# The output projection of the last layer in token parts of 384 and 136, with shorter roots and unused matmuls ahead of the last spread

## The chip, the cores and the metric

The kernel runs on one core of a Trainium2 chip. The metric is the device time of one execution in microseconds (us). Three runs of the kernel before took 1245.64, 1245.87 and 1247.6 us, median 1245.87. Each trace comes from one execution, taken by the hardware profiler.

Names of the engines: PE is the tensor engine's matmuls, PEld its weight loads, DVE the vector engine, ACT the scalar engine, POOL GpSimd, SP the engine that issues most DMAs.

## The reference, cut to what matters

Two layers (`DEPTH = 2`), `D_MODEL = 1024`, 512 prompt tokens and 8 decode samples of one token. Each layer is

```python
mod = jax.nn.silu(c) @ w_ada + b_ada
shift, scale, gate = jnp.split(mod[:, None, :], 3, axis=-1)
h = rmsnorm(x, norm_w) * (1.0 + scale) + shift
proj = h @ w_in                      # 1024 -> 7 * 1024
...
merged = jax.nn.sigmoid(gm) * y_m + jax.nn.sigmoid(gc) * y_c
x = x + gate * (merged @ w_out)
```

with an mLSTM branch (`y_m`) and a causal convolution branch (`y_c`) between. After the second layer a last `rmsnorm(x, final_norm_w)` gives the outputs for prompt and samples:

```python
def rmsnorm(x, w):
    xf = x.astype(jnp.float32)
    r = lax.rsqrt(jnp.mean(xf * xf, axis=-1, keepdims=True) + EPS)
    return (xf * r).astype(x.dtype) * w
```

## The kernel before, in words

Everything is held feature-major: a tile has 128 features on the partitions and the 520 tokens (512 prompt tokens, then the 8 samples) along the free axis; `KT = 8` such tiles make the 1024 features.

*Dense products.* `dense` (L178) makes one output tile of 128 features: for each of two token halves of 260 (`HALF`) it runs, over the 8 input tiles, three matmuls into one PSUM bank. Three, because weights and activations are split in a high and a low part of type fp32r (`whi`, `wlo`; `mh`, `ml` in the last stage), and high x high, high x low and low x high are summed. Each matmul is 128x128 weights by 260 columns, and each loads its weights anew. `split_w` (L161) brings a pair of weight tiles by DMA (`raw`, two buffers), casts the high part on ACT and subtracts the low part on POOL in four pieces of 256 columns. High and low land in rotating buffers (`WB = 3`), or in given places.

*Order.* The program is written in stages; a scheduler that simulates the engines sets each engine's order, within the dependencies and some `issue_after` hints. An engine runs its instructions in that order and waits at the first whose inputs are missing.

*The last stage* (`last_out`, L334) is the output projection of the second layer together with the final norm. For each output tile `m` and half `c`, `half` (L342) runs the 24 matmuls, adds the gated product to the old `x` on DVE (`residual`, L323; for the second half the samples need two more small instructions), squares on ACT, adds the squares up over the tiles on POOL (`presum`, into `total`) and multiplies by the norm weight on ACT. The tiles 0 to 3 run both halves in turn. The tiles 4 to 7 run their first halves first, then their second halves, so that the first half's norm can be made and written while the second halves are multiplied (`M_SPLIT = 4`). Since tiles 4 and 5 are used twice at a distance, their weights lie in buffers of the tag `k`, which the step before frees (`place`, L380).

*The norm of a half.* For the last tile the squares and `total` are summed over the partitions by matmuls with ones into four groups of 32 partitions (L352, `rmsn`), so that each instruction of the root works on 65 columns instead of 260. `inv_rms` (L357) scales the sum on DVE and takes the root: `rsqrt` (L149) starts with an integer guess and makes three Newton steps of three instructions. With the scaling (`var`) the root is eleven DVE instructions. `spread` (L362) brings the four groups back to all partitions with four matmuls (`frb`; fp32 matmuls appear as two records each) and copies the result to SBUF on ACT (`rbs`). `write` (L371) multiplies six tiles on DVE from PSUM and two on POOL from SBUF, and SP writes them to `o_y` in pairs. The pair (4, 5) of the first half is multiplied on DVE only after the last residual.

*Other uses of the root.* `rstd_of` (L224) calls it with 130 columns for the norm at the start of each layer (spread: `rb`) and for the convolution branch's layer norm (`lrb`); `norm_scales` calls it with 17 columns for the heads' norms of the mLSTM.

*The start.* While the first weights arrive, the sums of the first norm (`rms`) and the modulation `w_ada` (`ada`, chunks of four weight pieces that come one after the other by DMA, turned by `adat`) run on PE. Twelve unused matmuls of the identity (`idle`, L431) stand behind the first spread `rb`.

Of the kernel before, what the change touches and what calls it, by code (L numbers as in the profile page):

```python
# [42 lines left out]
T5B = 4  # L43
KO = 6
N_IDLE = 12
M_SPLIT = 4
F_GM = 7
F_Z = 11
F_ZL = 0
# [24 lines left out]
def build(nc, tc, ctx, ap):  # L74
# [55 lines left out]
    def pm(name, tag="m", bufs=3):  # L130
        return psp.tile([128, 512], F32, tag=tag, bufs=bufs, name=name)
# [17 lines left out]
    def rsqrt(vv, shape, tag):  # L149
        yi = sml.tile(shape, I32, tag="yi" + tag, bufs=1, name="yi")  # L150
        t = sml.tile(shape, F32, tag="yt" + tag, bufs=1, name="yt")
        y = yi.bitcast(F32)
        v.tensor_scalar(out=yi, in0=vv.bitcast(I32), scalar1=-0.5, scalar2=1597463007.0,
                        op0=ALU.mult, op1=ALU.add)
        for _ in range(3):
            v.tensor_tensor(out=t, in0=y, in1=y, op=ALU.mult)
            v.scalar_tensor_tensor(out=t, in0=t, scalar=-0.5, in1=vv, op0=ALU.mult, op1=ALU.mult)
            v.scalar_tensor_tensor(out=y, in0=t, scalar=1.5, in1=y, op0=ALU.add, op1=ALU.mult)
        return y

    def split_w(src, n, w=1024, place=(None, None)):  # L161
# [13 lines left out]
            out.append((hi, lo))  # L175
        return out

    def dense(w, xh, xl, nk, evac, halves=(0, 1)):  # L178
        hi, lo = w
        for c in halves:  # L180
            p = pm("pd", "d")
            n = 0
            for k in range(nk):
                ws = slice(k * 128, (k + 1) * 128)
                for a, b in ((hi, xh), (hi, xl), (lo, xh)):
                    mm = te.matmul(p[:, 0:HT], a[:, ws], b[:, k, HALF[c]], start=(n == 0), stop=(n == 3 * nk - 1))  # L186
# [135 lines left out]

    def residual(x, xo, mod, m):  # L323
        def ev(c, p):
            n = HT if c is HALF[0] else HT - TS
            v.scalar_tensor_tensor(out=x[:, m, c.start:c.start + n], in0=p[:, 0:n], scalar=mod[:, 16 + m, 0:1],  # L326
                                   in1=xo[:, c.start:c.start + n], op0=ALU.mult, op1=ALU.add)
            if n < HT:
                ts_ = sml.tile([128, TS], F32, tag="ots", bufs=2, name="ots")
                v.tensor_tensor(out=ts_, in0=p[:, n:HT], in1=mod[:, 16 + m, 1:9], op=ALU.mult)  # L330
                ev.last = v.tensor_tensor(out=x[:, m, TP:T], in0=ts_, in1=xo[:, TP:T], op=ALU.add)
        return ev

    def last_out(x, x_src, mod, mh, ml):  # L334
        accs = [pm("rmsn"), pm("rmsn")]
        total = s8.tile([128, T], F32, tag="s4", bufs=2, name="total")
        w = {}
        xo = big.tile([128, KT, T], F32, tag="u", name="xo")
        for k in range(0, KT, 2):
            nc.sync.dma_start(xo[:, k:k + 2], x_src[:, k:k + 2])  # L340

        def half(m, c):  # L342
            ev = residual(x, xo[:, m], mod, m)
            dense(w[m], mh, ml, KT, ev, (c,))
            sq = t520("sqo")
            s.activation(sq[:, HALF[c]], x[:, m, HALF[c]], AF.Square)
            if m < KT - 1:
                presum(total, sq, m == 0, HALF[c])
            else:
                for src in (total, sq):  # L350
                    for j in range(4):
                        te.matmul(accs[c][32 * j:32 * j + 32, 0:ET], ones[:, 0:32],  # L352
                                  src[:, (4 * c + j) * ET:(4 * c + j + 1) * ET], start=(src is total), stop=(src is sq))
            s.activation(x[:, m, HALF[c]], x[:, m, HALF[c]], AF.Copy, scale=fnw[:, m:m + 1])
            return ev

        def inv_rms(c):  # L357
            var = sml.tile([128, ET], F32, tag="var", bufs=1, name="var")
            v.tensor_scalar(out=var, in0=accs[c][:, 0:ET], scalar1=1.0 / D, scalar2=EPS, op0=ALU.mult, op1=ALU.add)
            return rsqrt(var, [128, ET], "q")  # L360

        def spread(r):  # L362
            p = pm("frb")
            for j in range(4):
                te.matmul(p[:, j * ET:(j + 1) * ET], ident[:, 32 * j:32 * j + 1].to_broadcast([128, 128]), r,
                          start=True, stop=True)
            rbs = t520("rbs")
            s.copy(rbs[:, 0:HT], p[:, 0:HT])
            return p, rbs

        def write(c, p, rbs, order):  # L371
            for k0 in order:
                for k in (k0, k0 + 1):
                    if k < 6:
                        v.tensor_tensor(out=x[:, k, HALF[c]], in0=x[:, k, HALF[c]], in1=p[:, 0:HT], op=ALU.mult)
                    else:
                        g.tensor_tensor(out=x[:, k, HALF[c]], in0=x[:, k, HALF[c]], in1=rbs[:, 0:HT], op=ALU.mult)
                nc.sync.dma_start(ap["o_y"][:, k0:k0 + 2, HALF[c]], x[:, k0:k0 + 2, HALF[c]])
# [33 lines left out]
    for l in range(L):  # L412
# [821 lines left out]
```

## Time and profile before

| | us |
|---|---|
| median of three runs | 1245.87 |
| the profiled execution: time | 1245.75 |
| its span, first to last instruction | 1244.0 |
| PE busy in the span | 1207.4 |
| PEld busy | 1161.5 |
| DVE busy | 850.7 |
| POOL busy | 648.6 |
| ACT busy | 550.0 |

All times in the profile count from the start of the span. PE rows are matmuls, PEld rows weight loads; both are pipelined, so their durations overlap, and the pace of a run is read from one start to the next. A row in order of time has the start, the length, the engine, the line, and the tiles out<-in. In the list of groups a row ends with busy time and mean nanoseconds of one, then the idle time ahead of them and what ended it. In the chain of waits a row has the start, the length and what ran. In a table of stretches each engine has its busy time and count, and the last three numbers are the granted clock of PE, the share of the DMA engines and GB/s.

### The profile page before, as it was taken

What the parts mean: (1) busy time and instruction counts of PE and PEld (TensorE: products, weight loads), DVE (VectorE), ACT (ScalarE), POOL (GpSimd) and SP (SyncE); (2) the same over time, 40 slices, a digit from 0 to 9 for tenths busy, and PEclk for the clock granted to TensorE, in tenths of its full rate; (3) what the DMA queues carried; (4) which work ended last, traced back from release to release, by engine and by line L of the source; (5) the groups of instructions that cost most, each with busy time, mean ns of one, the idle gap of its engine ahead of it and who ended that gap; (6) DMA issues with size and microseconds to landing.
All of it is one profiled execution on the core that took longest, in us unless ns stands there. A gap on an engine that the chain in (4) does not pass through costs nothing.

```text
span 1244.0 us, 26981 instructions
## 1 busy us (share of the span) xinstructions
PE 1207.4 (97%) x10856; PEld 1161.5 (93%) x10856; DVE 850.7 (68%) x1719; ACT 550.0 (44%) x991; POOL 648.6 (52%) x869
## 2 busy tenths in 40 slices
PE   6999999999999999999999999999999999999996
PEld 5999898899999999999988988988999999999995
DVE  6874467676998896654258635667789999937424
ACT  4676556543422223532236656556333222335242
POOL 2575444457544444565627553555665544536571
PEclk9999999999999999999999999999999999999998
DMA  9423447742364242243913234575332222224222
GB/s 362 148 89 94 146 149 256 266 173 95 104 219 153 91 148 86 78 170 130 366 67 96 87 109 175 195 263 213 125 103 94 94 88 100 86 85 137 104 86 69
DMA packets 59934, 177.23 MB, mean 142 GB/s; under 512 B 13408, under 2 KB 21664, under 8 KB 55712
## 3 DMA queue, kind: packets, MB, share of 16 engines
q1 hardware_dynamic: 56928, 167.08, 38.8%
q10 hardware_dynamic: 2880, 8.42, 1.8%
q8 instruction: 85, 1.39, 0.5%
q14 instruction: 41, 0.34, 0.1%
HBM read 149.77 MB, written 25.71 MB: 141 GB/s over the span
## 4 chain that ended last, share of the span: by engine, by line
PE 87%; DVE 4%; issue 3%; ACT 3%; DMA 2%; POOL 1%; SPq 0%; DVEq 0%; ACTq 0%; POOLq 0%
PE pd L186 72%; PE pds L889 3%; PE ppv L855 2%; PE pcf L855 2%; DMA wada<-w_ada 1%; PE ada L293 1%; PE ptok L850 1%; ACT whi L171 1%; PE pqc L789 1%; POOL wlo L174 1%; PE pg L688 1%; PE pd L246 1%; DMA raw<-wst 1%; PE pth L946 1%; PE pu L885 0%
## 5 line engine op out<-in xcount | busy, mean ns | idle before, releaser
L174 POOL TENSOR_TENSOR wlo<-raw,whi 128x256 fp32r<-128x256 f32 x680 | 523.8, 803 | 498.9 <-ACT whi L171 490.5
L186 PE MATMUL pd<-hh,whi 128*128 128x260 f32 x1728 | 494.9, 287 | 0.0
L186 PE MATMUL pd<-hl,whi 128*128 128x260 f32 x1728 | 492.2, 285 | 0.0
L186 PE MATMUL pd<-hh,wlo 128*128 128x260 f32 x1728 | 491.8, 285 | 0.0
L171 ACT CAST whi<-raw 128x1024 fp32r<-128x1024 f32 (+1 forms) x174 | 179.4, 1032 | 365.2 <-PE pd L186 329.7
L186 PEld LDWEIGHTS pd<-hh,whi 128*128 128x128 f32 x1728 | 326.8, 189 | 3.6 <-issue 1.8
L186 PEld LDWEIGHTS pd<-hh,wlo 128*128 128x128 f32 x1728 | 326.9, 189 | 1.8 <-issue 1.2
L186 PEld LDWEIGHTS pd<-hl,whi 128*128 128x128 f32 x1728 | 326.5, 189 | 1.8 <-issue 0.6
L535 DVE SCALAR_TENSOR_TENSOR cv<-u,vec,cv 128x509 f32<-128x509 f32 (+6 forms) x448 | 296.8, 729 | 0.0
L804 DVE SCALAR_TENSOR_TENSOR cb<-vb,wsk,cb 128x257 f32<-128x257 f32 x128 | 75.0, 651 | 1.1 <-ACT cb L802 0.4
L186 PE MATMUL pd<-hmh,whi 128*128 128x260 f32 x256 | 72.3, 282 | 0.0
L186 PE MATMUL pd<-hml,whi 128*128 128x260 f32 x256 | 72.3, 282 | 0.0
L186 PE MATMUL pd<-hmh,wlo 128*128 128x260 f32 x256 | 72.3, 282 | 0.0
L186 PE MATMUL pd<-zl,whi 128*128 128x260 f32 x256 | 71.6, 282 | 0.0
L186 PE MATMUL pd<-zh,wlo 128*128 128x260 f32 x256 | 71.6, 282 | 0.0
L186 PE MATMUL pd<-zh,whi 128*128 128x260 f32 x256 | 71.4, 282 | 0.0
L186 PE MATMUL pd<-mh,whi 128*128 128x260 f32 x224 | 63.1, 282 | 0.0
L186 PE MATMUL pd<-mh,wlo 128*128 128x260 f32 x224 | 63.1, 282 | 0.0
L186 PE MATMUL pd<-ml,whi 128*128 128x260 f32 x224 | 63.1, 282 | 0.0
L326 DVE SCALAR_TENSOR_TENSOR xr<-pd,mod,xo 128x260 f32<-128x260 f32 (+1 forms) x32 | 14.8, 482 | 60.7 <-PE pd L186 33.6
L186 PE MATMUL pd<-xcs,whi 128*128 128x260 f32 x256 | 48.5, 289 | 1.0
L186 PEld LDWEIGHTS pd<-hmh,wlo 128*128 128x128 f32 x256 | 48.2, 188 | 0.0
(304 smaller groups left out, 2236.7 us busy)
## 6 DMA issues: line engine op xcount, KB each, us to landing
raw<-wst SPq DMA_DIRECT2D x160, 512.0 KB, 3.7
wada<-w_ada SPq DMA_DIRECT2D x36, 512.0 KB, 9.1
cb<-C SPq DMA_DIRECT2D x16, 1028.0 KB, 7.8
o_C_s<-cb SPq DMA_DIRECT2D x16, 1028.0 KB, 5.7
vb<-vsc SPq DMA_DIRECT2D x16, 514.0 KB, 6.3
wada<-w_ada ACTq DMA_DIRECT2D x12, 512.0 KB, 8.0
raw<-wqkv SPq DMA_DIRECT2D x8, 512.0 KB, 3.6
x<-x SPq DMA_DIRECT2D x4, 520.0 KB
```

Of the source, the lines that this page charges most:

```text
L171: s.copy(hi, sl)
L174: g.tensor_tensor(out=lo[:, cs], in0=sl[:, cs], in1=hi.bitcast(F32)[:, cs], op=ALU.subtract)
L186: mm = te.matmul(p[:, 0:HT], a[:, ws], b[:, k, HALF[c]], start=(n == 0), stop=(n == 3 * nk - 1))
L246: mm = te.matmul(p[:, 0:HT], a[:, ws], b[:, k, HALF[c]], start=(k == 0 and i == 0), stop=(k == KT - 1 and i == 2))
L293: mm = te.matmul(acc[32 * j:32 * j + 32, 0:128], cT[:, k, :], raw[k // 2][:, k % 2, j * 128:(j + 1) * 128], start=(n == 0), stop=(n == KT ...
L326: v.scalar_tensor_tensor(out=x[:, m, c.start:c.start + n], in0=p[:, 0:n], scalar=mod[:, 16 + m, 0:1], in1=xo[:, c.start:c.start + n], op0= ...
L535: v.scalar_tensor_tensor(out=acc[a][:, sft:TP], in0=u[:, k, 0:TP - sft], scalar=wcol(sft), in1=acc[a][:, sft:TP], op0=ALU.mult, op1=ALU.add)
L688: te.matmul(pgs[n][32 * j:32 * j + 32, 0:HT], vec[:, o:o + 32], (q, kk, vv)[t][:, k, c], start=(r == 0), stop=(r == 5))
L789: te.matmul(p[32 * h:32 * h + 32, 0:V1], zq[:, o:o + 32], cb[:, k, :], start=(j == 0), stop=(j == 1))
L804: v.scalar_tensor_tensor(out=cb[:, 2 * h + j, :], in0=vb[:, h, :], scalar=wsk[:, h, j, b:b + 1], in1=cb[:, 2 * h + j, :], op0=ALU.mult, op ...
L855: te.matmul(p, a, b, start=(first and n == 0), stop=(last and n == 2))
L889: te.matmul(p[:, 0:n], kk[:, 2 * h + j, t0:t0 + 128], q[:, 2 * h + j, t0:TP], start=(j == 0), stop=(j == 1))
```

## The change

Four things change.

1. In the last stage the tokens are cut in 384 and 136 (`T_LAST`) instead of 260 and 260, and six tiles instead of four (`M_SPLIT`) run their second part last. The weights of tiles 2 to 5 lie in buffers of the tags `k` and `v`. The root of the first part works on 96 columns, that of the second on 34.
2. `rsqrt` makes one step of third order (four instructions) and one Newton step (three) instead of three Newton steps (nine). A constant factor of the new step is folded into a scale of its input (`RS = 64/9`), which the callers put into instructions that they have, but for `norm_scales`, which gets one more. With `var` a root is nine DVE instructions.
3. Eight unused matmuls of the identity (`N_END`) stand on PE between the last sums and the last spread.
4. The first part's pair (4, 5) is written, in the program, ahead of the last root.

```diff
+RS = 64.0 / 9
-M_SPLIT = 4
+M_SPLIT = 6
+T_LAST = 384
+N_END = 8
...
     def rsqrt(vv, shape, tag):
...
-        for _ in range(3):
-            v.tensor_tensor(out=t, in0=y, in1=y, op=ALU.mult)
-            v.scalar_tensor_tensor(out=t, in0=t, scalar=-0.5, in1=vv, op0=ALU.mult, op1=ALU.mult)
-            v.scalar_tensor_tensor(out=y, in0=t, scalar=1.5, in1=y, op0=ALU.add, op1=ALU.mult)
+        v.tensor_tensor(out=t, in0=y, in1=y, op=ALU.mult)
+        v.tensor_tensor(out=t, in0=t, in1=vv, op=ALU.mult)
+        v.scalar_tensor_tensor(out=t, in0=t, scalar=-10.0 / 3, in1=t, op0=ALU.add, op1=ALU.mult)
+        v.scalar_tensor_tensor(out=y, in0=t, scalar=5.0, in1=y, op0=ALU.add, op1=ALU.mult)
+        v.tensor_tensor(out=t, in0=y, in1=y, op=ALU.mult)
+        v.scalar_tensor_tensor(out=t, in0=t, scalar=-0.5 / RS, in1=vv, op0=ALU.mult, op1=ALU.mult)
+        v.scalar_tensor_tensor(out=y, in0=t, scalar=1.5, in1=y, op0=ALU.add, op1=ALU.mult)
         return y
...
-    def dense(w, xh, xl, nk, evac, halves=(0, 1)):
+    def dense(w, xh, xl, nk, evac, halves=(0, 1), split=HALF):
...
+            cols = split[c]
+            out = p[:, 0:cols.stop - cols.start]
...
     def last_out(x, x_src, mod, mh, ml):
...
+        LAST = (slice(0, T_LAST), slice(T_LAST, T))
+        LN = tuple((c.stop - c.start) // 4 for c in LAST)
...
         def place(i):
             if KT - M_SPLIT <= i < KT - 2:
                 b = i - (KT - M_SPLIT)
-                return tuple(big.tile([128, 2, T], F32R, tag=f"k{2 * b + j}", name="wk").rearrange("p a t -> p (a t)")
-                             for j in range(2))
+                return tuple(big.tile([128, 2, T], F32R, tag=f"{'kv'[b // 2]}{b % 2 * 2 + j}",
+                                      name="wk").rearrange("p a t -> p (a t)") for j in range(2))
...
-        half(4, 1)
+        for m in range(KT - M_SPLIT, KT - 3):
+            half(m, 1)
         r = inv_rms(0)
         half(5, 1)
-        pr = spread(r)
+        pr = spread(0, r)
         half(6, 1)
-        write(0, *pr, (0, 2, 6))
+        write(*pr, (0, 2, 6))
         ev = half(7, 1)
+        idle = pm("idle", "cv", 2)
+        with tc.issue_after(half.mm.ins):
+            for _ in range(N_END):
+                te.matmul(idle[:, 0:128], ident, ident, start=True, stop=True)
+        with tc.issue_after(ev.last.ins):
+            write(*pr, (4,))
         r = inv_rms(1)
-        with tc.issue_after(ev.last.ins):
-            write(0, *pr, (4,))
-        write(1, *spread(r), (0, 2, 6, 4))
+        write(*spread(1, r), (0, 2, 6, 4))
...
         def norm_scales():
...
+            v.tensor_scalar(out=dn, in0=dn, scalar1=RS, scalar2=None, op0=ALU.mult)
             y = rsqrt(dn, [128, NG], "g")
```

Since the root has fewer instructions everywhere, the scheduler's order changes at other places too. PE at the start of the kernel, before (`ada` are the matmuls of a modulation chunk, 32 for each; `rb` is the first spread; `adat` turns the first chunk):

```order
L193 MATMUL rms<-sq,ones 32x130 x32
L293 MATMUL ada<-wada,cT 32x128 x32
L201 MATMUL rb<-yi,ident 128x130 x4
L431 MATMUL idle<-ident 128x128 x6
L302 MATMUL adat<-ident,asb 128x128
L431 MATMUL idle<-ident 128x128 x6
L293 MATMUL ada<-wada,cT 32x128 x32
L246 MATMUL pd<-hh,whi 128x260
```

And PE at the same place now:

```order
L201 MATMUL rms<-sq,ones 32x130 x32
L301 MATMUL ada<-wada,cT 32x128 x24
L209 MATMUL rb<-yi,ident 128x130 x4
L451 MATMUL idle<-ident 128x128 x6
L301 MATMUL ada<-wada,cT 32x128 x8
L451 MATMUL idle<-ident 128x128 x6
L301 MATMUL ada<-wada,cT 32x128 x8
L310 MATMUL adat<-ident,asb 128x128
L301 MATMUL ada<-wada,cT 32x128 x24
L254 MATMUL pd<-hh,whi 128x260 x2
```

The spread has moved ahead of the first chunk's last quarter, and the transpose `adat` behind the first quarter of the second chunk.

DVE at the end of the last stage, before, from the last residual (L326 to L331) on:

```order
L326 SCALAR_TENSOR_TENSOR xr<-pd,mod,xo 128x252
L330 TENSOR_TENSOR ots<-pd,mod 128x8
L331 TENSOR_TENSOR xr<-ots,xo 128x8
L375 TENSOR_TENSOR xr<-xr,frb 128x260 x2
L359 TENSOR_SCALAR var<-rmsn 128x65
L153 TENSOR_SCALAR yi<-var 128x65
L156 TENSOR_TENSOR yt<-yi 128x65
L157 SCALAR_TENSOR_TENSOR yt<-yt,var 128x65
L158 SCALAR_TENSOR_TENSOR yi<-yt,yi 128x65
```

And now:

```order
L334 SCALAR_TENSOR_TENSOR xr<-pd,mod,xo 128x128
L338 TENSOR_TENSOR ots<-pd,mod 128x8
L339 TENSOR_TENSOR xr<-ots,xo 128x8
L390 TENSOR_TENSOR xr<-xr,frb 128x384 x2
L372 TENSOR_SCALAR var<-rmsn 128x34
L156 TENSOR_SCALAR yi<-var 128x34
L158 TENSOR_TENSOR yt<-yi 128x34
L159 TENSOR_TENSOR yt<-yt,var 128x34
L160 SCALAR_TENSOR_TENSOR yt<-yt 128x34
L161 SCALAR_TENSOR_TENSOR yi<-yt,yi 128x34
L162 TENSOR_TENSOR yt<-yi 128x34
L163 SCALAR_TENSOR_TENSOR yt<-yt,var 128x34
```

The two multiplies of the first part's pair (4, 5) stand ahead of the root in both; they are wider now, and everything behind them narrower.

PE at the end, before (`mh`, `ml` are the merged activations, `frb` the last spread):

```order
L186 MATMUL pd<-mh,whi 128x260
L186 MATMUL pd<-ml,whi 128x260
L186 MATMUL pd<-mh,wlo 128x260
L352 MATMUL rmsn<-total,ones 32x65 x4
L352 MATMUL rmsn<-sqo,ones 32x65 x4
L365 MATMUL frb<-yi,ident 128x65 x4
```

And now:

```order
L194 MATMUL pd<-mh,whi 128x136
L194 MATMUL pd<-ml,whi 128x136
L194 MATMUL pd<-mh,wlo 128x136
L365 MATMUL rmsn<-total,ones 32x34 x4
L365 MATMUL rmsn<-sqo,ones 32x34 x4
L419 MATMUL idle<-ident 128x128 x8
L379 MATMUL frb<-yi,ident 128x34 x4
```

The matmuls have kept their number and lost or gained columns, and the unused ones stand between the sums and the spread.

More of the change, by code (lines that the diff above doesn't have):

```diff
@@ L185, in dense @@
                 for a, b in ((hi, xh), (hi, xl), (lo, xh)):
-                    mm = te.matmul(p[:, 0:HT], a[:, ws], b[:, k, HALF[c]], start=(n == 0), stop=(n == 3 * nk - 1))
+                    mm = te.matmul(out, a[:, ws], b[:, k, cols], start=(n == 0), stop=(n == 3 * nk - 1))
                     n += 1
-            evac(HALF[c], p[:, 0:HT])
+            evac(cols, out)
         return mm
@@ L225, in rstd_of @@
         var = sml.tile([128, QT], F32, tag="var", bufs=1, name="var")
-        v.tensor_scalar(out=var, in0=acc[:, 0:QT], scalar1=1.0 / D, scalar2=EPS, op0=ALU.mult, op1=ALU.add)
+        v.tensor_scalar(out=var, in0=acc[:, 0:QT], scalar1=RS / D, scalar2=RS * EPS, op0=ALU.mult, op1=ALU.add)
         return rsqrt(var, [128, QT], "q")
@@ L324, in ev @@
         def ev(c, p):
-            n = HT if c is HALF[0] else HT - TS
+            n = min(c.stop, TP) - c.start
             v.scalar_tensor_tensor(out=x[:, m, c.start:c.start + n], in0=p[:, 0:n], scalar=mod[:, 16 + m, 0:1],
                                    in1=xo[:, c.start:c.start + n], op0=ALU.mult, op1=ALU.add)
-            if n < HT:
+            if c.stop == T:
                 ts_ = sml.tile([128, TS], F32, tag="ots", bufs=2, name="ots")
-                v.tensor_tensor(out=ts_, in0=p[:, n:HT], in1=mod[:, 16 + m, 1:9], op=ALU.mult)
+                v.tensor_tensor(out=ts_, in0=p[:, n:n + TS], in1=mod[:, 16 + m, 1:9], op=ALU.mult)
                 ev.last = v.tensor_tensor(out=x[:, m, TP:T], in0=ts_, in1=xo[:, TP:T], op=ALU.add)
@@ L340, in last_out @@
             nc.sync.dma_start(xo[:, k:k + 2], x_src[:, k:k + 2])
+        LAST = (slice(0, T_LAST), slice(T_LAST, T))
+        LN = tuple((c.stop - c.start) // 4 for c in LAST)
         def half(m, c):
             ev = residual(x, xo[:, m], mod, m)
-            dense(w[m], mh, ml, KT, ev, (c,))
+            cols = LAST[c]
+            dense(w[m], mh, ml, KT, ev, (c,), split=LAST)
             sq = t520("sqo")
-            s.activation(sq[:, HALF[c]], x[:, m, HALF[c]], AF.Square)
+            s.activation(sq[:, cols], x[:, m, cols], AF.Square)
             if m < KT - 1:
-                presum(total, sq, m == 0, HALF[c])
+                presum(total, sq, m == 0, cols)
             else:
@@ L351, in half, with spread @@
                     for j in range(4):
-                        te.matmul(accs[c][32 * j:32 * j + 32, 0:ET], ones[:, 0:32],
-                                  src[:, (4 * c + j) * ET:(4 * c + j + 1) * ET], start=(src is total), stop=(src is sq))
-            s.activation(x[:, m, HALF[c]], x[:, m, HALF[c]], AF.Copy, scale=fnw[:, m:m + 1])
+                        o = cols.start + j * LN[c]
+                        half.mm = te.matmul(accs[c][32 * j:32 * j + 32, 0:LN[c]], ones[:, 0:32], src[:, o:o + LN[c]],
+                                            start=(src is total), stop=(src is sq))
+            s.activation(x[:, m, cols], x[:, m, cols], AF.Copy, scale=fnw[:, m:m + 1])
             return ev
         def inv_rms(c):
[L358 to L362, printed above, removed]
+            var = sml.tile([128, LN[c]], F32, tag="var", bufs=1, name="var")
+            v.tensor_scalar(out=var, in0=accs[c][:, 0:LN[c]], scalar1=RS / D, scalar2=RS * EPS, op0=ALU.mult, op1=ALU.add)
+            return rsqrt(var, [128, LN[c]], "q")
+        def spread(c, r):
             p = pm("frb")
+            n = LN[c]
             for j in range(4):
-                te.matmul(p[:, j * ET:(j + 1) * ET], ident[:, 32 * j:32 * j + 1].to_broadcast([128, 128]), r,
+                te.matmul(p[:, j * n:(j + 1) * n], ident[:, 32 * j:32 * j + 1].to_broadcast([128, 128]), r,
                           start=True, stop=True)
             rbs = t520("rbs")
-            s.copy(rbs[:, 0:HT], p[:, 0:HT])
-            return p, rbs
+            s.copy(rbs[:, 0:4 * n], p[:, 0:4 * n])
+            return c, p, rbs
         def write(c, p, rbs, order):
+            cols, n = LAST[c], 4 * LN[c]
             for k0 in order:
@@ L374, in write @@
                     if k < 6:
-                        v.tensor_tensor(out=x[:, k, HALF[c]], in0=x[:, k, HALF[c]], in1=p[:, 0:HT], op=ALU.mult)
+                        v.tensor_tensor(out=x[:, k, cols], in0=x[:, k, cols], in1=p[:, 0:n], op=ALU.mult)
                     else:
-                        g.tensor_tensor(out=x[:, k, HALF[c]], in0=x[:, k, HALF[c]], in1=rbs[:, 0:HT], op=ALU.mult)
-                nc.sync.dma_start(ap["o_y"][:, k0:k0 + 2, HALF[c]], x[:, k0:k0 + 2, HALF[c]])
+                        g.tensor_tensor(out=x[:, k, cols], in0=x[:, k, cols], in1=rbs[:, 0:n], op=ALU.mult)
+                nc.sync.dma_start(ap["o_y"][:, k0:k0 + 2, cols], x[:, k0:k0 + 2, cols])
         def place(i):
```

## The prediction

> **What bounds the kernel now.** I read the page first, then the chain of waits over the last stage, then the instructions in order of time around its end.
>
> ```profile
> span 1244.0 us, 26981 instructions
> PE 1207.4 (97%) x10856; PEld 1161.5 (93%) x10856; DVE 850.7 (68%) x1719; ACT 550.0 (44%) x991; POOL 648.6 (52%) x869
> ```
>
> TensorE is the bound, and the weight loads (PEld) are almost as full as the matmuls. The chain of waits from 1183 us on (start, length, what):
>
> ```profile
> 1182.89 35.36 PE pd L186 x296
> ...
> 1227.04 0.84 PE frb L365 x8
> 1227.88 2.23 PE pd L186 x18
> ...
> 1230.14 0.48 DVE xr L326
> ...
> 1231.46 0.36 PE rmsn L352 x8
> ...
> 1231.85 0.24 DVE var L359
> ...
> 1234.82 1.95 PE frb L365 x8
> ...
> 1236.85 0.39 ACT rbs L368
> ...
> 1238.02 1.34 DVE xr L375 x4
> ```
>
> Up to 1230.12 (1227.88 + 2.23) the chain is matmuls alone: 296 in 35.36 us, 0.1195 us each. So TensorE never waits in the output stage, whose 384 matmuls of 260 columns take 384 x 0.1195 = 45.9 us. From 1230.12 to 1244.0 lies a tail of 13.9 us in which TensorE hardly works: last residual, square, sums, root, spread, multiply, write. The change touches both halves of this picture.
>
> **The matmuls of the last stage.** Before, each output tile is 24 matmuls of 260 columns twice, 48 x 0.1195 = 5.74 us. Now it is 24 of 384 and 24 of 136 columns; the columns add up to the same 520. If time followed columns alone, nothing would change. So I look for narrow matmuls of this kind (fp32r operands, a new 128x128 weight each) in the trace. There are some in the score step:
>
> ```profile
> 167.73 0.22 PE L885 MATMUL pu<-ur,selr 128*128 128x128 f32 x1
> 167.74 0.19 PEld L887 LDWEIGHTS pu<-mneg,identr 128*128 128x128 f32 x1
> 167.79 0.27 PE L887 MATMUL pu<-mneg,identr 128*128 128x128 f32 x1
> 167.84 0.19 PEld L186 LDWEIGHTS pd<-hh,whi 128*128 128x128 f32 x1
> 167.90 0.34 PE L186 MATMUL pd<-hh,whi 128*128 128x260 f32 x1
> 167.95 0.19 PEld L186 LDWEIGHTS pd<-hl,whi 128*128 128x128 f32 x1
> 168.08 0.28 PE L186 MATMUL pd<-hl,whi 128*128 128x260 f32 x1
> ```
>
> The first matmul of 128 columns starts 0.06 us ahead of the next: its own weights were loaded in good time. But the weight loads start at 167.74, 167.84 and 167.95, 0.10 to 0.11 us apart however short the matmul between them is, and the debt shows at once: the second narrow matmul takes 0.11 us, and the 260-column one after it 0.18 instead of 0.12. The three take 0.35 us, which is 0.11 + 0.11 + 0.12. A longer run of narrow ones is the spread ahead of the last tile:
>
> ```profile
> 1226.77 0.97 PEld L365 LDWEIGHTS frb<-yi,ident 128*128 128x128 f32 x8
> 1226.88 1.00 PE L365 MATMUL frb<-yi,ident 128*128 128x65 f32 x8
> ```
>
> Eight loads of 0.19 us in 0.97 us: (0.97 - 0.19) / 7 = 0.111 us apart, for matmuls of 65 columns. So a 128x128 weight load has a pace of 0.111 us, and no stream of matmuls with new weights runs faster. At 260 columns it is just hidden; at 136 it is not. For the wide part I take a 512-column matmul of the same kind:
>
> ```profile
> 187.96 0.39 PE L885 MATMUL pu<-ur,selr 128*128 128x512 f32 x1
> 188.19 0.22 PE L887 MATMUL pu<-mneg,identr 128*128 128x128 f32 x1
> ```
>
> 512 columns take 0.23 us start to start, 260 take 0.1195; on the line between them 384 take 0.1195 + 124/252 x 0.11 = 0.173 us. Bounds: 0.165 (nearly in proportion to columns from the lower end) and 0.178. For 136 columns the bounds are 0.062 (in proportion to 260) and 0.1195 (no narrow one can cost more than a wide one); I take 0.111, as both rows say so. The stage then takes 8 x 24 x (0.173 + 0.111) = 54.5 us, against 45.9: **+8.6 us**.
>
> [...]
>
> That six instead of four tiles have their second part last costs nothing by itself: the two more pairs of weight tiles lie in buffers that the step before frees, and GpSimd's splitting, which must keep ahead, is 4 x 0.8 us a tile:
>
> ```profile
> L174 POOL TENSOR_TENSOR wlo<-raw,whi 128x256 fp32r<-128x256 f32 x680 | 523.8, 803 | 498.9 <-ACT whi L171 490.5 <-PE pd L186 4.8 <-DMA raw<-wst 3.6
> L222 POOL TENSOR_TENSOR total<-total,sqo 128x260 f32<-128x260 f32 x12 | 8.9, 749 | 13.3 <-ACT sqo L346 13.3
> ```
>
> A first part brings it 3.2 us of that and a sum of squares (0.75 us for 260 columns, 1.1 for 384), 4.3 us against TensorE's 24 x 0.173 = 4.2. Even without any lead six such tiles would cost under 1 us, and the full tiles ahead of them (6.8 us each) give a lead.
>
> **The tail.** Its steps, with 1.04 ns a column on VectorE from these rows (554 - 287 over 256 columns), and ScalarE taken as the same:
>
> ```profile
> L895 DVE TENSOR_TENSOR dd<-dd,pds 128x384 f32<-128x384 f32 x8 | 4.4, 554 | 5.1 <-PE pds L889 5.1
> L895 DVE TENSOR_TENSOR dd<-dd,pds 128x128 f32<-128x128 f32 x8 | 2.3, 287 | 3.4 <-PE pds L889 2.8
> ```
>
> - Last residual, 252 to 128 columns: -0.13. The square is shorter by 0.1 too, but the two multiplies of the first part that stand ahead of the root grow from 260 to 384 columns (+0.26 for two) and end last instead. So -0.13 in all.
> - Root: eleven instructions with `var`, from 1231.85 to the spread at 1234.82, are 2.97 us, 0.27 each. Nine of 34 instead of 65 columns: 9 x (0.27 - 0.03) = 2.15. -0.8.
> - Spread: 1.95 us here, 0.84 to 1.00 us for the same eight records at 1226.88. The difference is the clock (last column but two is PEclk):
>
> ```profile
> 1230.45:1233.80 3.35, 0.64 (x16) 0.32 (x16) 2.79 (x13) 0.93 (x2) 0.13 (x1) 1.00 0.85 282
> 1233.90:1237.00 3.10, 1.94 (x8) 1.78 (x8) 0.68 (x3) 0.15 (x1) 0.00 (x0) 0.50 0.00 0
> ...
> 151.90:155.20 3.30, 1.01 (x9) 1.00 0.58 177
> 155.30:158.60 3.30, 3.30 (x16) 0.50 0.96 370
> ```
>
> After 3.35 us with 0.64 us of work the granted clock is halved; the same follows 1.01 us of work in 3.3 at 152 us. The eight unused matmuls are 16 records at 0.111 us, 1.8 us:
>
> ```profile
> 16.99 1.50 PE L431 MATMUL idle<-ident 128*128 128x128 f32 x12
> ```
>
> (1.50 us for 12, the last 0.275 long.) They start when the sums end, so they lie under the root's 2.15 us and are over some 0.3 us ahead of the spread: free. With them TensorE is at work for over half of the time from its last real matmul to the spread. If the clock holds, the spread is shorter by 1.95 - 1.0: -0.95. If it does not, this gain is gone, and the unused matmuls, at half speed 3.6 us, end 3.6 - 2.15 = 1.45 us after the root.
> - ScalarE's copy and six multiplies, 260 to 136 columns: 7 x 0.13 = -0.9.
> - The last four writes, 260 KB each, now 136 KB:
>
> ```profile
> 1229.17 11.04 SPq L378 DMA_DIRECT2D o_y<-xr  x8
> ...
> GB/s 0 0 0 0 0 0 0 0 0 0 0 0 0 0 78 338 359 296 380 333 328 380 317 328 374 348 328 364 364 317 94 0 0 0 0 0 0 0 0 41
> ```
>
> Each slice is 0.2 us; 16 of them, 3.2 us, run at about 340 GB/s, so these transfers stand in a queue for the DMA engines: 0.78 us each, and the last issue, over at 1240.2, is ahead of their end. Half the bytes halve that to 1.6 us, but each write's issue and latency remain. Between 0 and -1.6; I take -1.2.
>
> Sum of the tail: -0.13 - 0.8 - 0.95 - 0.9 - 1.2 = **-4.0 us** (-4.7 to -1.5).
>
> **The other roots.** A shorter root also moves the order elsewhere. At the start TensorE's queue now has the last quarter of the first modulation chunk behind the spread, and the transpose behind a matmul group of the second chunk:
>
> ```profile
> 18.33 0.27 PE L302 MATMUL adat<-ident,asb 128*128 128x128 f32 x1
> ...
> 19.43 1.52 ACT L439 ACTIVATE hh<-x,mod,sa 128x512 fp32r<-128x512 f32 x2 [0.34 <-DVE sa L308]
> 19.89 0.65 PE L293 MATMUL ada<-wada,cT 128*32 128x128 f32 x16
> ...
> 23.56 0.70 DVE L321 TENSOR_TENSOR hl<-hs,hh 128x16 fp32r<-128x16 f32 x1
> ...
> 24.15 0.39 PE L246 MATMUL pd<-hh,whi 128*128 128x260 f32 x1
> ```
>
> The group that starts at 19.89 waits for its weights, so the transpose moves from 18.33 to 19.89 + 0.65 = 20.5, and ScalarE's and VectorE's preparation of the first tiles with it, by 2.2 us. The last of it (`hl` of the sample columns, over at 24.26) would be over at about 25.8 to 26.4, where TensorE, which before had its first twelve matmuls done by 24.15 + 12 x 0.12 = 25.6, still has five to do. I take +0.6 (0 to +1.3): part of the 2.2 us was slack, and the multiplies that GpSimd slows before 24.9 are then faster. At the second layer's start the root was last:
>
> ```profile
> 632.68 1.13 PE L201 MATMUL rb<-yi,ident 128*128 128x130 f32 x8 [0.37 <-DVE yi L158]
> L201 PE MATMUL lrb<-yi,ident 128*128 128x130 f32 x16 | 2.1, 275 | 0.0
> ```
>
> Two instructions fewer take those 0.37 us: -0.4 (0 to -0.7). The layer norm's root (`lrb`, idle 0.0) is covered by the gate tiles' matmuls: 0; without that cover it would be worth two instructions, 0.7 us. The state norm's root loses two and gains one: 0.
>
> **Sum**, against the profiled execution (1245.75 us, of which 1244.0 are the span): 8.6 - 4.0 + 0.6 - 0.4 = +4.8, so 1250.6 us. The median of the runs shown is 1245.87, 0.1 above it: 1250.7 us. A measurement can tell about 0.2%, 2.5 us, from no change.
>
> **Rivals.**
> - *The narrow loads hide* (the other side). If weight loads and narrow matmuls overlap fully, 136 columns take 0.062 us, the stage stays within 0.7 us of 45.9 (192 x 0.235 = 45.1), and the tail's gain is left: 1245.9 - 0.8 - 4.0 + 0.2 = 1241.3. It decides at 0.239 - 0.173 + 3.8/192 = 0.086 us for 136 columns: below that the change is not slower. For it: one start-to-start of 0.06 us at 167.73. Against: the loads' 0.11 us right behind.
> - *Half hidden*: a load starts early enough that half of the excess is covered, (0.062 + 0.111) / 2 = 0.087 us. The stage is 192 x 0.26 = 49.9 us: 1245.9 + 4.0 - 4.0 + 0.2 = 1246.1, no change. For it, the first narrow matmul of a run does have its load hidden; against it, the eight loads of the spread, of which none does after the first. [...]
> - *The clock falls ahead of the last spread all the same*: 0.95 + 1.45 us of the tail's gain are lost, 1253.1. For it: nothing but the two stretches above says how much work keeps the clock. [...]
>
> **How the numbers follow.** Chances: forecast 0.80, loads hide 0.06, half hidden 0.06, clock falls 0.08. Within the forecast the terms' bounds are +6.4 to +10 for the stage, -4.7 to -1.5, 0 to +1.3 and -0.7 to 0; not all at one end at once, so 1248 to 1254, and the low end reaches to 1247 for part of the half-hidden cases; the clock's 1253.1 lies inside. Slower by over 0.2% (above 1248.4): most of the forecast and the clock case, 0.85. Within: half hidden and the forecast's lower edge, 0.09. Faster: 0.06.
>
> **What would show it.** In the changed profile: 24 matmuls of 136 columns start 0.11 us apart and their weight loads likewise (0.06 or 0.08: I am wrong); 384 columns 0.17 apart; stage of 54 to 55 us without a wait; PEclk 1.00 in the last spread, about 1 us long; nine VectorE instructions in about 2 us; under 10.5 us from the last such matmul to the end; at the start the transpose near 20.5. A stage near 46 us makes the forecast wrong, whatever the tail does.

## The result, and the profile after

The changed kernel took 1251.76 us (median of four executions, 1251.47 to 1253.81), the kernel before 1245.84 beside it. The ratio is 1.0053, 95% interval 1.0039 to 1.0067. The change is slower by 5.9 us, more than the 0.2% that a measurement can tell. The profiled execution took 1251.86 us, its span is 1250.1 us; that is 6.1 us over the span of before.

The heads of its page:

```profile
span 1250.1 us, 26994 instructions
PE 1219.7 (98%) x10872; PEld 1173.4 (94%) x10872; DVE 843.3 (67%) x1705; ACT 548.7 (44%) x991; POOL 646.7 (52%) x869
```

TensorE has 16 records more (the unused matmuls), but 12.3 us more of busy time, and so have the weight loads (11.9). VectorE has 7.4 us less. The stage's first matmuls and its last one, in the view in order of time, of the changed kernel:

```profile
1181.92 0.34 PE L194 MATMUL pd<-mh,whi 128*128 128x384 f32 x1
1182.10 0.35 PE L194 MATMUL pd<-ml,whi 128*128 128x384 f32 x1
...
1238.66 0.28 PE L194 MATMUL pd<-mh,wlo 128*128 128x136 f32 x1
```

and of the kernel before:

```profile
1182.25 0.28 PE L186 MATMUL pd<-mh,whi 128*128 128x260 f32 x1
...
1229.82 0.28 PE L186 MATMUL pd<-mh,wlo 128*128 128x260 f32 x1
```

From the first start to the last are 56.74 us now and 47.57 before: the stage is 9.2 us longer. (Both hold the first part's sums and spread, 1.51 us now and 1.34 before.) The chain of waits from there on:

```profile
1222.18 0.30 PE rmsn L365 x8
1222.48 2.27 PE pd L194 x19
1224.75 0.30 PE rmsn L365 x8
1225.05 7.63 PE pd L194 x67
1232.68 0.91 PE frb L379 x8
1233.60 5.36 PE pd L194 x48
...
1238.98 0.35 DVE xr L334
...
1239.69 0.33 ACT sqo L358
...
1240.06 0.27 PE rmsn L365 x8
1240.33 3.37 PE idle L419 x16
1243.71 1.07 PE frb L379 x8
...
1244.85 0.28 ACT rbs L382
```

There is no wait in the stage: matmul follows on matmul. The last 48, all of 136 columns, take 5.36 us, 0.1117 each. With the sums and the spread taken off (0.30 + 0.30 + 0.91), the 192 wide ones have (56.74 - 1.51 - 192 x 0.1117) / 192 = 0.176 us. The 0.1117 us is not a pace of issuing: the modulation's matmuls (`ada`), whose weights have only 32 columns, come under 0.03 us apart (96 in 2.80 us in the kernel before, from 625.82 on).

The tail runs from 1238.96 to 1250.1, 11.1 us against 13.9. But in the middle of its chain stands not VectorE's root: there stand the unused matmuls, 3.37 us long. The root's first and last instruction:

```profile
1240.45 0.19 DVE L372 TENSOR_SCALAR var<-rmsn 128x34 f32<-128x34 f32 x1
...
1242.26 0.20 DVE L164 SCALAR_TENSOR_TENSOR yi<-yt,yi 128x34 f32<-128x34 f32 x1
```

It is over at 1242.46, after 2.0 us, and the spread can only follow at 1243.71, when the unused matmuls are over. The table of stretches says why (the last column but two is the granted clock):

```profile
1233.82:1237.24 3.42, 3.42 (x33) 3.42 (x32) 2.54 (x7) 0.88 (x3) 2.41 (x3) 1.00 0.33 117
1237.25:1240.67 3.42, 2.50 (x35) 2.26 (x34) 1.62 (x7) 1.22 (x4) 0.47 (x1) 1.00 0.63 231
1240.67:1244.09 3.42, 3.42 (x19) 3.42 (x18) 1.55 (x8) 0.00 (x0) 0.00 (x0) 0.50 0.32 115
```

At 1240.67 the clock is halved for 3.42 us, though TensorE was busy for 2.50 of the 3.42 us before (PE's column, the first behind the length).

### The profile page after: what moved, and what is told of

Read it like the earlier page. It is cut to its first block, busy times and chain, and to the rows that moved or that the text cites. A ratio compares the mean times of both kernels' runs of the same rounds, so it can differ in the third digit from the quotient of the medians.

```text
span 1250.1 us, 26994 instructions
## 1 busy us (share of the span) xinstructions
PE 1219.7 (98%) x10872; PEld 1173.4 (94%) x10872; DVE 843.3 (67%) x1705; ACT 548.7 (44%) x991; POOL 646.7 (52%) x869
## 4 chain that ended last, share of the span: by engine, by line
PE 86%; DVE 4%; DMA 3%; issue 3%; ACT 3%; POOL 1%; SPq 0%; DVEq 0%; ACTq 0%; POOLq 0%
PE pd L194 73%; PE pds L910 2%; PE ppv L876 2%; PE pcf L876 2%; DMA wada<-w_ada 2%; PE ada L301 1%; PE ptok L871 1%; ACT whi L177 1%; DMA cb<-C 1%; DVE cb L824 1%; PE pg L708 1%; PE pd L254 1%; PE pqc L809 1%; POOL wlo L180 1%; PE pth L967 1%
## 5 line engine op out<-in xcount | busy, mean ns | idle before, releaser
L180 POOL TENSOR_TENSOR wlo<-raw,whi 128x256 fp32r<-128x256 f32 x672 | 514.9, 797 | 496.7 <-ACT whi L177 496.5
L334 DVE SCALAR_TENSOR_TENSOR xr<-pd,mod,xo 128x260 f32<-128x260 f32 (+3 forms) x32 | 15.3, 484 | 69.3 <-PE pd L194 47.1
L194 PE MATMUL pd<-ml,whi 128*128 128x260 f32 (+2 forms) x192 | 55.7, 291 | 0.0
L194 PE MATMUL pd<-mh,whi 128*128 128x260 f32 (+2 forms) x192 | 55.6, 291 | 0.0
L194 PE MATMUL pd<-mh,wlo 128*128 128x260 f32 (+2 forms) x192 | 55.5, 290 | 0.0
```

Source lines behind the costliest of these rows:

```text
L180: g.tensor_tensor(out=lo[:, cs], in0=sl[:, cs], in1=hi.bitcast(F32)[:, cs], op=ALU.subtract)
L194: mm = te.matmul(out, a[:, ws], b[:, k, cols], start=(n == 0), stop=(n == 3 * nk - 1))
```

## The experiments

The theory from this profile: every matmul needs at least the 0.111 us of its weight load, so parts of 136 columns are paid like parts of 240, and this alone is the loss. Its rivals: a fixed cost plus columns; the other order and the six tiles. For the tail there are two: the clock is granted by the share of time in which columns stream through TensorE (a narrow matmul that waits for its weights is under way, but streams little), or it is lost by gaps between matmuls.

The ratio is to the kernel before on the same chip. The stage is read from the first start of its matmuls to the last; the tail from the end of the last one to the end of the span.

| kernel | ratio (95%) | stage us | tail us |
|---|---|---|---|
| before | 1 | 47.57 | 13.9 |
| changed | 1.0053 (1.0039 to 1.0067) | 56.74 | 11.1 |
| changed, second profile | 1.0054 (1.0041 to 1.0067) | 56.74 | 10.0 |
| parts 260 and 260 | 0.9986 (0.9975 to 0.9997) | 47.56 | 12.1 |
| 320 and 200 | 1.0015 (1.0002 to 1.0028) | 51.28 | 11.0 |
| 280 and 240 | 0.9993 (0.9982 to 1.0004) | 47.95 | 11.7 |
| 240 columns, 136 used | 1.0045 (1.0032 to 1.0058) | 56.96 | 10.0 |
| parts alone (with the six tiles) | 1.0056 (1.0042 to 1.0070) | 56.74 | 11.7 |
| roots alone | 0.9995 (0.9985 to 1.0006) | 47.54 | 12.5 |
| no unused matmuls | 1.0047 (1.0032 to 1.0062) | 56.74 | 10.8 |
| 260 and 260, none unused | 0.9990 (0.9981 to 0.9999) | 47.57 | 12.0 |
| wide unused matmuls | 1.0043 (1.0029 to 1.0057) | 56.74 | 10.0 |
| 260 and 260, four last | 0.9984 (0.9973 to 0.9995) | 47.54 | 12.2 |

### The parts back to 260 and 260

```diff
-T_LAST = 384
+T_LAST = 260
```

> Changed kernel with parts of 260 and 260, all else kept (six second parts last, short roots, unused matmuls). Theory weight-load pace (a matmul never takes less than the 0.111 us of its weight load, so 136 columns cost almost what 260 do): the stage goes back to 384 x 0.1195 = 45.9 us from 55.1, the tail gets some 1.5 us longer (copy, multiplies, writes of 260 columns), total about 1244 us, faster than both kernels. Rival, the stage grew through the six tiles with second parts last and their weights in other buffers: the stage stays above 50 us, total 1248 us or more.

Measured: 1244.46 us, 0.9986 of the kernel before. The stage is 47.56 us, as before, though six tiles still have their second part last. So the rival that puts the loss on the six tiles or their buffers is out: the loss is in the widths.

### 320 and 200

```diff
-T_LAST = 384
+T_LAST = 320
```

> Changed kernel with parts of 320 and 200. Weight-load pace: 200 columns 0.111 us like 136, 320 columns 0.147 us (on the line 0.1195 at 260, 0.176 at 384), stage 192 x 0.258 = 49.5 us, total about 1247 us. Rival, a fixed cost plus columns (line through 0.111 at 136 and 0.1195 at 260): 200 columns 0.1154 us, stage 50.4 us, total about 1248. Rival, time in proportion to columns from the 260 row: 200 columns 0.092 us, stage 45.9 us, total about 1243.5.

Measured: 1247.96 us; the stage is 3.7 us over that of 260 and 260 (forecast by the load pace 3.6, by the fixed cost 4.5, in proportion 0). The last 48 matmuls, from the chain of waits:

```profile
1230.92 5.40 PE pd L194 x48
```

0.1125 us each for 200 columns, 0.1117 for 136.

### 240 columns multiplied, 136 used

```diff
+            n = cols.stop - cols.start
+            wide = slice(min(cols.start, T - 240), cols.stop)
+            run = p[:, 0:wide.stop - wide.start]
+            out = p[:, wide.stop - wide.start - n:wide.stop - wide.start]
...
-                    mm = te.matmul(out, a[:, ws], b[:, k, cols], start=(n == 0), stop=(n == 3 * nk - 1))
+                    mm = te.matmul(run, a[:, ws], b[:, k, wide], start=(n == 0), stop=(n == 3 * nk - 1))
```

> Changed kernel, but the matmuls of each second part run over 240 columns, of which only the last 136 are used (104 columns multiplied for nothing). Weight-load pace: 240 columns fit under a load of 0.111 us, so the stage stays at 55.1 us although 20% more columns are multiplied. Rival, fixed cost plus columns: 0.118 us each, stage 56.5 us. On the clock: if what holds it is the share of time in which columns stream, the second parts now stream almost all the time, the granted clock stays 1.00 behind the last sums, the unused matmuls take 1.8 us instead of 3.4, and the total is about 1250.5 us; if it is the gap of 0.9 us between the sums, the clock falls as before and the total is 1251.8 us (1253.2 by the rival).

Measured: 1251.97 us, ratio 1.0045. The second parts stream 76% more columns, and the stage is longer by 0.2 us (56.96 against 56.74). From the chain of waits:

```profile
1234.68 5.42 PE pd L197 x48
```

0.1129 us each. The columns between 136 and 240 are nearly free: what is paid is not the columns, and the weight load, which each matmul has besides, fits the figure. The table of stretches answers the other question, on the clock:

```profile
1238.10:1241.51 3.41, 2.48 (x35) 2.21 (x33) 1.35 (x5) 1.36 (x4) 0.47 (x1) 1.00 0.71 258
1241.51:1244.92 3.41, 3.03 (x24) 2.73 (x24) 1.82 (x10) 0.18 (x2) 0.00 (x0) 1.00 0.32 115
```

As busy as the changed kernel's stretch (2.48 against 2.50 us), with the same gap ahead of the last sums, and the clock stays at 1.00 behind it. By an estimate with the 0.46 ns a column from the row of widths below, the matmuls here, up to 1240.10, stream for nearly all of their time (0.110 of 0.113 us), those there for little over half of it (0.063 of 0.112). The tail is 10.0 us. Together with the row of widths below this speaks for the share of streaming.

### Without the unused matmuls

```diff
-N_END = 8
+N_END = 0
```

> Changed kernel without the eight unused matmuls. Theory: they ran at half clock and ended 1.25 us behind the root; without them the spread starts when the root is over, but at half clock takes 1.95 us instead of 1.07, so the tail goes from 11.15 to about 10.8 us, total about 1251.5, no difference that can be measured. Rival, they do hold the clock: the spread alone gets longer and the tail grows to 12.0 us, total 1252.7.

Measured: 1252.4 us, ratio 1.0047, not to be told from the changed kernel. In its profile the spread starts right behind the root (1245.66) and at half clock takes 1.92 us:

```profile
1243.26 0.27 PE L365 MATMUL rmsn<-sqo,ones 128*32 128x34 f32 x8 [0.93 <-ACT sqo L358]
1245.71 1.92 PE L379 MATMUL frb<-yi,ident 128*128 128x34 f32 x8 [2.18 <-DVE yi L164]
```

The tail is 10.8 us, as expected. What the unused matmuls save on the spread (0.85 us) they give back in the profiled execution by ending 1.25 us behind the root.

### A row of widths

```diff
-            for _ in range(N_END):
-                te.matmul(idle[:, 0:128], ident, ident, start=True, stop=True)
+            for n, m in ((384, 24), (256, 24), (240, 24), (200, 24), (136, 24), (64, 96), (512, 24)):
+                for _ in range(m):
+                    te.matmul(idle[:, 0:n], identr, ur[:, 0:n], start=True, stop=True)
```

> Changed kernel in which the eight unused matmuls are replaced by rows of unused fp32r matmuls, each with a 128x128 load of its own: 24 each of 384, 256, 240, 200 and 136 columns, 96 of 64, 24 of 512. Only the pace of each row is read; the total grows by some 30 us. Weight-load pace: 384 take 0.176 us, 256 0.118, and 240, 200, 136 and 64 all 0.111. Fixed cost plus columns: 240 0.118, 200 0.115, 136 0.111, 64 0.106. Half hidden: 136 near 0.083, 64 less. On the clock: if it follows the share of time in which columns stream, the 96 matmuls of 64 columns (10.7 us without a gap, columns streaming for a quarter of it) halve it; if it follows gaps between matmuls, it stays at 1.00.

Measured, one profile. The groups of four rows that lie at full clock (busy time, mean ns of one):

```profile
L420 PE MATMUL idle<-ur,identr 128*128 128x256 f32 x24 | 3.0, 281 | 0.0
L420 PE MATMUL idle<-ur,identr 128*128 128x240 f32 x24 | 2.8, 274 | 0.0
L420 PE MATMUL idle<-ur,identr 128*128 128x200 f32 x24 | 2.8, 274 | 0.0
L420 PE MATMUL idle<-ur,identr 128*128 128x136 f32 x24 | 2.8, 274 | 0.0
```

Busy time less the last record's, by 23: (2.8 - 0.274) / 23 = 0.110 us for 240, 200 and 136 columns alike (0.110 to 0.112 from their starts), 0.118 for 256. The 64 columns start 0.112 apart as long as the clock is full, and 0.213 at half clock: the floor nearly doubles. This is the cost by itself, with nothing to wait for. And the clock, over the end of the row of 136 and into that of 64:

```profile
1252.90:1256.31 3.41, 3.41 (x34) 3.41 (x32) 0.00 (x0) 0.00 (x0) 0.00 (x0) 1.00 0.00 0
1256.31:1259.72 3.41, 3.41 (x33) 3.41 (x32) 0.00 (x0) 0.00 (x0) 0.00 (x0) 1.00 0.00 0
1259.72:1263.13 3.41, 3.41 (x18) 3.41 (x17) 0.00 (x0) 0.00 (x0) 0.00 (x0) 0.50 0.00 0
```

33 matmuls of 64 columns touch the stretch from 1256.31 on, 34, most of them of 136 columns, the one before: a load's pace, again. TensorE is busy for 3.41 of 3.41 us, and yet the clock is halved behind it. So the clock can be halved without a gap. A column costs (0.176 - 0.1195) / 124 = 0.00046 us, so 64 columns stream, by this estimate, for a quarter of 0.11 us, and 136 for 0.56 of it: here a stretch at a quarter lost the clock, and the one before it, most of it 136 columns, kept it.

### The shorter roots alone

The kernel before, with the new `rsqrt` and its scales and nothing else:

```diff
+RS = 64.0 / 9
...
-        for _ in range(3):
...
+        v.scalar_tensor_tensor(out=t, in0=t, scalar=-10.0 / 3, in1=t, op0=ALU.add, op1=ALU.mult)
```

> Kernel before with the shorter roots alone. The last root loses two instructions of 0.27 us (-0.5), the second layer's start 0.4 us; the kernel's start costs +0.2 us (what the changed kernel's trace showed) or +0.6 (what was forecast). Total 0.3 to 0.7 us under the kernel before, less than can be measured. Rival: the new order of the start costs more than these gain, total 0 to 1 us over it.

Measured: 1245.87 us, 0.9995 with an interval that holds 1. By the profile the root takes 2.30 us instead of 2.82 (the -0.5 expected); the spread of that execution, 1.45 us from 1235.41, lay in part at full clock (until 1235.97), which is no work of the change. Inconclusive in the total, as so small a gain has to be.

### The parts alone

The changed kernel with the old `rsqrt`, without unused matmuls and with the last write of the first part in its old place:

```diff
-RS = 64.0 / 9
+RS = 1.0
-N_END = 8
+N_END = 0
```

> Kernel before with the parts of 384 and 136 and the six second parts last alone (long roots, no unused matmuls, old place of the pair (4, 5)). Weight-load pace: stage +9.1 us. Tail: residual and square -0.25, root eleven instructions of 34 columns -0.3, copy and multiplies -0.9, writes -1.2, the spread still at half clock: -2.7. Total 6.4 us over the kernel before. Rival, a good part of the changed kernel's loss comes from the new order that the shorter roots and the unused matmuls bring: 4 us over it or less.

Measured: 1253.24 us, ratio 1.0056, 7.1 us over the kernel before on that chip. The stage is 9.2 us longer; the tail is 11.7 us, 0.5 longer than expected. The whole loss is in the parts; what the other three edits together give back is less than these runs can tell (1.0053 with them, and the intervals overlap).

### 280 and 240

```diff
-T_LAST = 384
+T_LAST = 280
```

> Changed kernel with parts of 280 and 240, the narrowest second part that the weight-load pace does not punish: 280 columns 0.1287 us, 240 columns 0.111, stage 192 x 0.2397 = 46.0 us as before, and a tail 0.3 us shorter than with 260 and 260. Total 0.2 us under the version with halves, so about 2 us under the kernel before. Fixed cost plus columns: 240 columns 0.118 us, stage 47.4 us, total 1.1 us over the version with halves.

Measured: 1245.31 us, 0.9993. The stage is 0.4 us over that of the halves (0.1 expected; the 48 last matmuls take 5.44 us, 0.1133 each, between the two theories' 0.111 and 0.118), and the tail 0.4 us shorter. No gain over the halves.

### 260 and 260 without unused matmuls

```diff
-T_LAST = 384
-N_END = 8
+T_LAST = 260
+N_END = 0
```

> Parts of 260 and 260, short roots, six second parts last, without the unused matmuls. If these hold the clock for the spread, it now takes 1.95 us instead of 1.1 in most executions, and the total is 0.5 to 0.9 us over the version with halves and unused matmuls (0.9986 of the kernel before), so about the kernel before. If they are worth nothing, the ratio stays near 0.9986.

Measured: 1244.84 us, 0.9990 (0.9981 to 0.9999), against 0.9986 with them. The intervals overlap: a gain by the unused matmuls, if there is one, is under what these runs can tell. In its profile the clock fell only behind the spread (1.12 us long, as with them), without any unused matmul, so the tail is the same.

### Unused matmuls that stream

```diff
+                    if c and src is total:
+                        half.idle = pm("idle", "cv", 2)
+                        with tc.issue_after(half.mm.ins):
+                            for _ in range(3):
+                                te.matmul(half.idle, identr, ur, start=True, stop=True)
...
-                te.matmul(idle[:, 0:128], ident, ident, start=True, stop=True)
+                te.matmul(half.idle, identr, ur, start=True, stop=True)
```

> Changed kernel (384 and 136), but with unused matmuls in which columns stream all the time: three of 512 columns between the two halves of the last sums and eight of 512 columns behind them, in place of the eight of 128. Theory, the clock follows the share of streaming: it stays 1.00 up to the spread, the eight take 1.9 us, under the root of 2.0, and the tail from the last real matmul to the end is 10.1 us instead of 11.2; total up to 1 us under the changed kernel. Rival, the clock falls for another reason: the eight take up to 4.5 us at half clock, 2.5 us over the root, and the tail is 12.5 us or more.

Measured: 1251.92 us, ratio 1.0043; the changed kernel beside it on the same chip has 1252.97, 1.0054. In order of time, with L371 and L423 the unused ones:

```profile
1240.31 0.96 PE L371 MATMUL idle<-ur,identr 128*128 128x512 f32 x3
1241.31 0.27 PE L365 MATMUL rmsn<-sqo,ones 128*32 128x34 f32 x8
1241.51 2.13 PE L423 MATMUL idle<-ur,identr 128*128 128x512 f32 x8
1243.76 1.08 PE L384 MATMUL frb<-yi,ident 128*128 128x34 f32 x8
```

All at full clock, over at 1243.64, 0.06 us ahead of the root's end; the tail is 10.0 us. What is new is above all the three in the gap: the unused matmuls of 128 columns are of type fp32, a column of which takes 0.84 ns (last section), so they stream too, for 0.107 of the 0.112 us of their loads. It is as the theory has it, though one profile can't show that it holds in every execution, and the difference of 1 us in the medians is within the two intervals.

### Four second parts last, with 260 and 260

```diff
-M_SPLIT = 6
-T_LAST = 384
+M_SPLIT = 4
+T_LAST = 260
```

> Parts of 260 and 260, short roots, unused matmuls, but four second parts last as in the kernel before. Forecast: six instead of four costs and gains nothing by itself, so the ratio is that of the version with halves and six (0.9986) within 0.0005. Rival: six tiles give GpSimd or the writes more time, and four is 0.5 us or more slower.

Measured: 1244.16 us, 0.9984. Six or four is the same (0.9986 and 0.9984), as far as intervals of 0.0011 to each side can tell.

### The changed kernel again

> The changed kernel again, beside these on the same chip, as the base for the unused matmuls: ratio 1.0053 to the kernel before as measured, within 0.0014. With another phase of the clock's grid the unused matmuls take 1.8 or 3.4 us, and the tail 10.0 or 11.2 us.

Measured: 1252.97 us, 1.0054. In its profile the unused matmuls are over in time:

```profile
1244.21 2.05 PE L419 MATMUL idle<-ident 128*128 128x128 f32 x16
1246.45 1.08 PE L379 MATMUL frb<-yi,ident 128*128 128x34 f32 x8 [0.19 <-DVE yi L164]
```

and the last matmuls of the stage, in its chain of waits, are

```profile
1237.54 5.36 PE pd L194 x48
```

so its tail is 1252.9 - 1242.9 = 10.0 us. The stretch of the clock that holds the unused matmuls, and the next:

```profile
1242.64:1246.04 3.40, 2.47 (x35) 2.24 (x33) 2.85 (x13) 0.73 (x2) 0.00 (x0) 1.00 0.39 143
1246.05:1249.45 3.40, 1.29 (x10) 0.98 (x9) 1.64 (x8) 0.27 (x1) 0.90 (x2) 1.00 0.14 51
```

It is as busy as the one that lost the clock in the first profile (2.47 and 2.50 us, 35 records each, 16 of them the sums). But it has the 16 unused ones and 3 of 136 columns, and the other had 3 unused ones and 16 of 136 columns, which stream for only 0.06 us each (136 x 0.46 ns). So the same kernel has a tail of 11.1 or 10.0 us, by where a stretch of the clock happens to begin.

## Why the prediction was right, and where it was not

The forecast was 1250.7 us, measured are 1251.76. The likeliest case came, for the reason given: at 136 columns the weight load is what is paid.

- *The stage, +8.6:* +9.2. The mechanism was right; 136 columns take 0.1117 us (forecast 0.111). The term was short by 0.6 us because 384 columns take 0.176 us, not the 0.173 of the line drawn through 260 and 512; 192 x 0.003 is the 0.6. "The narrow loads hide" (0.062) and "half hidden" (0.087) are refuted by the row of widths: nothing from 64 to 240 columns is under 0.11.
- *Six tiles, 0:* right, as far as it can be told (0.9984 with four, 0.9986 with six).
- *The tail, -4.0:* -2.8 in the profiled execution. The step that failed is "over some 0.3 us ahead of the spread: free". The forecast took it that TensorE, being at work for over half of the time, keeps its clock, which was an estimate; but the clock fell behind a stretch that was busy for 2.50 of 3.42 us: being at work wasn't the measure. So the 16 records took 3.37 instead of 1.8 us (2.05 in the second profile, at full clock), and the spread waited 1.25 us for them. The rival "the clock falls" had this mechanism, at 1.45 us, but had the spread slow as well (0.95). It was not (1.07 us): the next stretch, from 1244.09, was granted in full; the slowed matmuls had filled the one before (3.42 of 3.42 us busy), which is probably why. In the second profile the clock held, and there the tail is 3.9 us shorter: the sum of -4.0 was right on its condition.
- *The single steps of the tail:* from the last matmul to `var` 1.49 us instead of 1.73 (-0.24, forecast -0.13); the root 2.0 from `var` to its end (2.15 forecast); the spread 1.07 (1.0); from `rbs` to the end 1250.1 - 1244.85 = 5.25 against 7.15, -1.9 (forecast -0.9 - 1.2 = -2.1).
- *The kernel's start, +0.6:* +0.2. The transpose moved as forecast, to 20.65 (20.5):

```profile
20.65 0.33 PE L310 MATMUL adat<-ident,asb 128*128 128x128 f32 x1
...
23.76 0.64 PE L301 MATMUL ada<-wada,cT 128*32 128x128 f32 x16 [0.61 <-DMA wada<-w_ada]
24.33 0.51 PE L254 MATMUL pd<-hh,whi 128*128 128x260 f32 x2
```

TensorE still waited last for a transfer of weights ahead of 23.76, and the first matmul came at 24.33 instead of 24.15: the preparation behind the transpose found its slack in that wait. Two multiplies of the sample columns in it (128x16 on VectorE) take 0.16 us each behind the end of GpSimd's split at 23.88; in the kernel before they took 0.70 each beside it (it ended at 24.92).
- *The second layer's start, -0.4:* -0.4. The spread there has no wait any more, and the distance of the two traces falls from 1.29 us ahead of it to 0.85 behind.

```profile
633.53 1.16 PE L209 MATMUL rb<-yi,ident 128*128 128x130 f32 x8
```

What the stage and the tail leave of the 6.1 us is 6.1 - 9.2 + 2.8 = -0.3, at the stage's start (1181.92 against 1182.25). It is made of start (+0.2) and second layer (-0.4), of small pieces that cancel, and of two things that the forecast didn't have: in this execution the matmuls of 260 columns between 504 and 625 us were a little slower (+0.85; why stays open), and a stretch of half clock that the kernel before had at 670.6 us is missing (-1.0). From the tables of stretches, before:

```profile
670.60:674.10 3.50, 3.44 (x16) 3.44 (x17) 3.50 (x7) 3.08 (x9) 2.93 (x5) 0.51 0.06 11
```

and after:

```profile
670.60:674.10 3.50, 2.02 (x17) 2.02 (x17) 3.50 (x7) 3.50 (x10) 2.55 (x4) 1.00 0.32 107
```

This doesn't belong to the change: in its second profile the clock is halved from 672.61 to 679.44, and the stage begins only at 1185.86.

So that the total came within 1.1 us of the forecast is in part luck: the stage's 0.6 and the tail's 1.2 us too much stand against 0.4 too little at the start, and the two things that nobody had forecast nearly cancel.

## What to carry to other kernels

A matmul that loads its own 128x128 weights has a price floor, here 0.111 us or some 240 columns of fp32r: cut a token axis so that no part is narrower than that, and a shorter tail has to be worth what the narrow part loses at every weight (0.049 us x 192 here). The versions that keep 260 and 260 and take the rest of the change are the best measured, 0.9984 and 0.9986 of the kernel before; the interval leaves out 1, but the gain is under 0.2%. Work put in to keep a clock up stands in the queue ahead of what it is to help: if the clock falls all the same, it takes longer (3.37 against 2.05 us here), and what it was to help waits for it (1.25 us). A row of 64 columns without a gap, streaming for an estimated quarter of its time, lost the clock all the same: here matmuls that are narrow against the time of their load were a poor filling.

## What the runs showed of the hardware

- The pace of fp32r matmuls with a 128x128 load each is 0.110 to 0.113 us at 136, 200 and 240 columns, 0.118 at 256, 0.1195 at 260 and 0.176 at 384. At half clock the row of 64 columns has 0.213.
- In the changed kernel's trace the clock is at 0.50 from 155.24 to 158.65, from 766.22 to 769.63 and from 1240.67 to 1244.09, for 3.41 us each time (and from 1247.50 to the end, where TensorE has nothing left). The distances of these starts are 179 and 139 times 3.413 us. The kernel before has the first two stretches at the same times. In the row of widths the clock falls at 1259.72, in the changed kernel's second profile at 672.61, and neither lies a whole number of 3.413 us from them: the grid can differ between executions. Busy time doesn't part the stretches that lost the clock from those that kept it: the gapless row of 64 columns, busy for 3.41 of 3.41 us, lost it, and a stretch mostly of 136 columns, as busy, kept it. In the changed kernel a stretch busy for 2.50 of 3.42 us, with a gap of 0.93 us, lost it; from 670.65 on one busy for 1.98 of 3.41 us, with a gap of 2.19 us ahead of 672.08, kept it. The share of streaming columns fits both pairs, by an estimate from 0.46 ns for a column of fp32r (row of widths) and 0.84 for one of fp32 (in the changed kernel's score step such matmuls of 512 and 256 columns start 0.429 and 0.216 us apart): a quarter against about half in the rows, and in the changed kernel about 0.4 (13 matmuls of 136 columns, three unused ones, and the sums, which start 0.01 us apart) against 0.56 (16 of 260). That this share alone decides was not shown, and no run was made for a limit. In the run with the row of widths even 1.65 us of busy time, all of it matmuls of 260 columns, kept the clock:

```profile
669.22:672.63 3.41, 1.65 (x13) 1.65 (x14) 3.41 (x7) 3.29 (x10) 2.17 (x3) 1.00 0.45 135
672.64:676.04 3.40, 3.40 (x31) 3.40 (x30) 3.40 (x6) 3.37 (x8) 2.96 (x5) 1.00 0.30 99
```

- Two executions of the changed kernel differ in where the clock is halved: its two profiles begin the last stage at 1181.92 and 1185.86 us, and 3.2 of these 3.9 us arise between 668.65 and 675.30, where the clock is halved in the second alone. Single executions of the kernel before lay between 1242.1 and 1249.0 us on one chip; how much of that is the clock wasn't measured. A change of 1 us in a tail is lost in that without many runs.
